# One transformer-like block on one core: early sums on every pair, the last pair behind five chunks, another order in the input norm

## The chip, the cores and the metric

The kernel runs on one core of a Trainium2 chip. The metric is the device time of one execution in microseconds (us); the kernel before takes 1717.28 us, the median of 3 runs (1715.68 to 1718.93).

## What is computed

The input x is a sequence of 1024 tokens of width 1024, in float32. One block is applied:

```
h  = rms_norm(x, norm_mix_g);  proj = h @ w_in            # 4 mixers' inputs, a and b of the delta net, 4 gates
merged = sum over 4 mixers of sigmoid(gate) * (mixer(...) @ w_br)
x  = x + merged @ w_out
h  = rms_norm(x, norm_ffn_g)
up = causal_conv3(h @ w_up) + conv_b;  val, gate = split(up)       # 2 x 2816 channels
x  = x + (silu(gate) * val) @ w_down                               # 2816 -> 1024
out = rms_norm(x, norm_final_g)
```

All matrix products keep float32 accuracy: each operand is split into a rounded high part and the rest (`hi`, `lo`), and every product of two blocks is three matmuls (hi*hi, lo*hi, hi*lo).

## The kernel before

The activations lie with channels on the 128 partitions and tokens along the free dimension, in two halves of 512 tokens (f = 0 and 1). Weights are streamed from memory in pieces of 128x512, 256 KB each, and split on the chip: ScalarE (ACT) makes the high part (L148), VectorE (DVE) or GpSimd (POOL) subtracts to get the low part (L155). Each engine works through its own queue in order. What stands in a queue before what is decided before the run by a list scheduler: of the instructions whose inputs it believes ready it takes the one that comes first in the program. So the order written in the code is a priority, and neighbouring steps are mixed. A queue can therefore hold an instruction that the scheduler thought ready and that is not.

**Input norm** (`norm_in`, L349 to L401). The norm needs the sum of squares of every token, which is late. So the first products run on unnormalised x*g, and their results are scaled afterwards by the row of inverse roots `rt`. For each half f: `scale_split` makes h_hi and h_lo; the products of the first delta-net block (`pd`) and of the 8 columns for a and b (`ab_products`) run; the squares are summed (`ssq`), `rms_scale` reduces them on TensorE and takes the inverse root in some twelve tiny DVE instructions (`rs1m`, `rs1a`, `rs1y` for f = 1); `spread_scale` spreads the result with 8 small matmuls and copies it to `rt` (L404). Two gate blocks are then multiplied (`pg`, `ps`, 24 matmuls each for one half), and `rescale` (L406) rewrites h of a half as the normalised one: eight times a DVE multiplication (L411), a cast on ACT and a subtraction (L155), the latter on DVE for k = 0, 3, 6 and on POOL for the other five. `ab_out` (L422) multiplies the a/b columns by `rt` (L426, tile `abf`), transposes them on TensorE (L96) and adds them up; the delta net's scalars start from that.

**Up projection** (`ffn_up`, L1598). 22 pairs i of blocks (a value block and a gate block), each a 2x2 block product done with seven instead of eight block products (`seven`): 84 matmuls of 512 columns a pair. TensorE writes the quarters of the result to the PSUM tiles `qa` and `qb`, of which there are two sets. Between the products DVE adds snapshots into them (L1587, L1589, L1591); the sixth product of a pair waits for L1587. `pair_weights` prepares the seven weight operands of the next pair, with nine POOL instructions a pair (L1545 to L1552 and L155). `hidden(i)` works on the finished pair: scaling by `rt` (L1617), a 3-tap convolution (L1618, L1620), the gate (L1627, L1628) and the product `val` (L1629), which is stored (`gd[i]`). For the down projection, which is a 2x2 block product with seven products as well, `hidden(i)` also makes sums and stores them: POOL computes and stores one difference of `val` (`td[0]`) for i < 11 and two (`td[1]`, `td[2]`) for i >= 11; and at every even i, with k = i/2, it loads three pieces of the down weights, and POOL computes and stores two sums of them, `sd[0][k]` (L1648) and `sd[1][k]` (L1650). The buffers `tu` for all this are five.

**Down projection** (`ffn_down`, L1677). Seven products of 11 chunks each; a chunk is two pieces of 128x512 (a weight w and a hidden-value piece x), two splits and 12 matmuls. The pieces land in a ring of eight raw slots (`raw_slot`), the split parts go to a ring of seven (`w_slot`, shared with the up projection's weights) or, with `own="t"`, x goes to six tiles of the pool `down`. The pool lies where the up projection's tiles were, so its first use waits until `hidden(21)` and its stores are through. The first product uses rings alone (`own=None`). From the 23rd piece on every even piece has a tile `raws` of the pool `down` (8 of them), and from the second product on x has its own tiles. `residual` loads the x to which the result is added, through POOL's queue. In the program the down projection comes after `hidden(21)`.

Of the kernel before, what the change touches and what calls it, by code (L numbers as in the profile page):

```python
# [21 lines left out]
P = 128  # L22
# [8 lines left out]
LEAD = 24  # L31
N_HELD = 6
# [66 lines left out]
class Builder:  # L99
# [249 lines left out]
    def norm_in(self):  # L349

        nc = self.nc
        with ExitStack() as st:
# [24 lines left out]
            for f, s in enumerate(halves):  # L377
                for k in range(NK):
                    self.scale_split(xs[f][:, k, :], g[:, k:k + 1], self.h_hi[:, k, s], self.h_lo[:, k, s], nc.vector)
                dn.append(self.products(self.early[B_DN], s, self.ps("pd")))  # L380
                ab = self.ab_products(w_ab, s)
                ssq = self.t(xp, [P, 512], F32, "ssq", 2)
                for k in range(NK):
                    x = xs[f][:, k, :]
                    sq = ssq if k == 0 else self.t(xp, [P, 512], F32, "rms_sq", 4)
                    nc.scalar.activation(sq, x, AF.Square)
                    if k:
                        nc.vector.tensor_tensor(ssq, ssq, sq, op=ALU.add)
                r = self.rms_scale(xp, ssq, self.ones, 1.0 / 1024, f"rs{f}")
                self.spread_scale(r, f)  # L390
                if f:
                    self.rescale(xs[0], g, 0)
                o = [self.products(self.early[B_GATE], s, self.gate_ps()), self.products(self.load_in(B_GATE + 1), s, self.ps())]
                if f:
                    self.rescale(xs[1], g, 1)
                for i in range(2):
                    self.gate_out(i, s, self.scaled(o[i], s))
                self.ab_out(xp, ab, s, f)
            self.started = {B_GATE + 2: [self.products(self.load_in(B_GATE + 2), halves[0], self.gate_ps())]}
            self.started[B_DN + 2] = [self.products(self.load_in(B_DN + 2), halves[0], self.ps())]  # L400
# [5 lines left out]
    def rescale(self, x, g, f):  # L406

        nc = self.nc
        s = slice(512 * f, 512 * f + 512)
        for k in range(NK):  # L410
            nc.vector.scalar_tensor_tensor(x[:, k, :], x[:, k, :], g[:, k:k + 1], self.rt[:, s], op0=ALU.mult, op1=ALU.mult)  # L411
            self.split(self.h_hi[:, k, s], self.h_lo[:, k, s], x[:, k, :], nc.scalar, nc.vector if k % 3 == 0 else nc.gpsimd)
# [972 lines left out]
    def build(self):  # L1385
# [44 lines left out]
        with ExitStack() as sx, ExitStack() as st:  # L1430
# [12 lines left out]
            with ExitStack() as s1:  # L1443
                self.ffn_up(ctx, sx, st, s1, xs, ssq, late)
        self.ffn_down(ctx)
# [152 lines left out]
    def ffn_up(self, ctx, sx, st, s1, xs, ssq, late):  # L1598
# [23 lines left out]
        def hidden(i, q):  # L1622
# [20 lines left out]
            if i % 2 == 0:  # L1643
                k = i // 2
# [3 lines left out]
                g.tensor_tensor(a21, a21, a22, op=ALU.add)  # L1648
# [22 lines left out]
        for i in range(1, N_FF):  # L1671
            j = job(i)
            for _ in j[2]:
                pass
            hidden(*j[:2])

    def ffn_down(self, ctx):  # L1677
# [3 lines left out]

        nc = self.nc
        v, g = nc.vector, nc.gpsimd
        pool = self.pool(ctx, "down", side="left")
# [4 lines left out]
        def raw(src):  # L1689
            i = next(n_raw)  # L1690
            r = flat(self.raw_slot("rffsrfsf"[i % 8])) if i < 2 * N_HALF or i % 2 else self.t(pool, [P, 512], F32, "raws", 8)
# [19 lines left out]
        def A(a, b):  # L1711
            return lambda k: self.a["w_dn"][N_HALF * b + k][:, halves[a]]
# [6 lines left out]
        G = [[x[:, h] for x in self.banks() for h in halves] for _ in range(2)]  # L1719
# [75 lines left out]
        product(G[0], [A(0, 0)], [B(0, 0)], True, own=None)  # L1795
        residual(0, 0)
        product(G[1], [A(0, 1)], [B(1, 0)], True, between={5: adds(0, 0, G[0]), 7: lambda: residual(1, 0)})
# [124 lines left out]
```

## Time and profile before

| | before |
|---|---|
| median of 3 runs | 1717.28 us (1715.68 to 1718.93) |
| the profiled execution's own time | 1719.06 us |
| its span, first to last instruction | 1717.3 us |
| TensorE (PE) busy | 1641.2 us, 96% |
| DVE / ACT / POOL busy | 1256.2 / 678.4 / 645.1 us |
| mean granted TensorE clock | 0.984 of full speed |

The profile is of one execution. Busy PE is the time in which a matmul is under way; it contains time at a lower clock. In the lists of instructions a row is start, duration (us), engine, line, operation, output<-inputs, shape, count; what stands in brackets is the idle time of the engine before the instruction and what ended it. A line can be that of a helper: L92 is every matmul, L148 the cast to the high part, L155 the subtraction for the low part.

### The profile page before, as it was taken

The numbers are of one execution on the slowest core, as the hardware profiler recorded it, in microseconds if no ns is written. First come the engines' busy times: TensorE is split into PE (matmuls) and PEld (weight loads), VectorE is DVE, ScalarE is ACT, GpSimd is POOL, SyncE is SP. The second block draws the span as 40 slices with busy tenths as digits, with TensorE's granted clock in tenths as the row PEclk, the third lists the DMA queues.
The fourth block names the chain that finished last, engine by engine and source line by source line (L and its number), as shares of the span: only waits on it lengthen the run. The fifth ranks groups of instructions, "written<-read, shape, count | busy, mean of one in ns | idle before, by whom it ended". The sixth has DMA issues, their size and how long they took to land.

```text
span 1717.3 us, 22540 instructions
## 1 busy us (share of the span) xinstructions
PE 1641.2 (96%) x7762; PEld 1321.3 (77%) x7762; DVE 1256.2 (73%) x2265; ACT 678.4 (40%) x1219; POOL 645.1 (38%) x571
## 2 busy tenths in 40 slices
PE   7899999989999999999999999999998989999996
PEld 5686776766787877778888787788887777778886
DVE  8895966777623749795578667888878888855785
ACT  4342332212332336564213445454443434444353
POOL 2412033344310222211001425988999898300002
PEclk9899999999999999999999999999999999999998
DMA  4113222213432673414755442433344344687763
GB/s 156 66 64 90 60 83 70 90 64 78 149 130 98 137 141 90 102 50 150 275 201 172 141 141 66 143 123 128 135 142 148 135 147 148 219 306 242 246 213 104
DMA packets 137955, 233.64 MB, mean 136 GB/s; under 512 B 42785, under 2 KB 51745, under 8 KB 137329
## 3 DMA queue, kind: packets, MB, share of 16 engines
q1 hardware_dynamic: 105072, 151.26, 28.4%
q10 hardware_dynamic: 17968, 54.37, 8.7%
q0 software_dynamic: 14800, 26.58, 6.0%
q8 instruction: 61, 1.00, 0.2%
q14 instruction: 54, 0.43, 0.1%
HBM read 164.69 MB, written 66.85 MB: 135 GB/s over the span
## 4 chain that ended last, share of the span: by engine, by line
PE 68%; DVE 10%; DMA 3%; issue 3%; POOL 2%; ACT 2%; SPq 0%; DVEq 0%; POOLq 0%; ACTq 0%
PE qb L92 16%; PE pd L92 15%; PE qa L92 14%; PE pg L92 13%; PE ps L92 6%; DVE glo L155 2%; PE ps L96 1%; PE p L92 1%; DVE cg L1628 1%; DMA fr<-sd 1%; DMA fr<-gd 1%; ACT p L1029 0%; DMA raws<-in_w_dn_dram 0%; POOL x L1772 0%; DVE wlo L155 0%
## 5 line engine op out<-in xcount | busy, mean ns | idle before, releaser
L155 POOL TENSOR_TENSOR glo<-raw,ghi 128x512 fp32r<-128x512 f32 x72 | 98.3, 1368 | 361.7 <-ACT ghi L148 348.5
L92 PE MATMUL pg<-hhi,ghi 128*128 128x512 f32 x496 | 207.2, 418 | 0.0
L92 PE MATMUL pg<-hlo,ghi 128*128 128x512 f32 x496 | 198.9, 401 | 0.0
L92 PE MATMUL pg<-hhi,glo 128*128 128x512 f32 x496 | 198.8, 401 | 0.0
L92 PE MATMUL pd<-hhi,whi 128*128 128x512 f32 x312 | 128.2, 412 | 2.0 <-ACT silt L511 1.9
L92 PE MATMUL pd<-hhi,wlo 128*128 128x512 f32 x312 | 122.4, 392 | 2.0 <-DVE wlo L155 2.0
L92 PE MATMUL pd<-hlo,whi 128*128 128x512 f32 x312 | 122.2, 392 | 0.0
L148 ACT CAST ghi<-raw 128x512 fp32r<-128x512 f32 x97 | 59.9, 618 | 152.6 <-DVE cv L1629 75.8
L92 PE MATMUL qa<-xh,ghi 128*128 128x512 f32 x264 | 105.4, 399 | 14.9 <-DVE qa L1587 14.9
L92 PEld LDWEIGHTS pg<-hhi,ghi 128*128 128x128 f32 x496 | 95.1, 192 | 23.1 <-issue 6.7
L92 PEld LDWEIGHTS pg<-hlo,ghi 128*128 128x128 f32 x496 | 95.2, 192 | 19.3
L92 PEld LDWEIGHTS pg<-hhi,glo 128*128 128x128 f32 x496 | 95.5, 192 | 15.8 <-issue 0.3
L92 PE MATMUL qa<-xh,glo 128*128 128x512 f32 x264 | 104.4, 395 | 0.0
L92 PE MATMUL qa<-xl,ghi 128*128 128x512 f32 x264 | 104.3, 395 | 0.0
L92 PE MATMUL qb<-xh,whi 128*128 128x512 f32 x264 | 103.1, 391 | 1.2 <-ACT whi L148 0.8
L92 PE MATMUL qb<-xh,wlo 128*128 128x512 f32 x264 | 102.7, 389 | 0.0
L92 PE MATMUL qb<-xl,whi 128*128 128x512 f32 x264 | 102.7, 389 | 0.0
L148 ACT CAST whi<-raw 128x512 fp32r<-128x512 f32 x90 | 55.9, 621 | 89.2 <-PE pd L92 53.4
L155 DVE TENSOR_TENSOR wlo<-raw,whi 128x512 fp32r<-128x512 f32 x61 | 46.7, 767 | 39.1 <-ACT whi L148 38.9
L92 PEld LDWEIGHTS pd<-hhi,whi 128*128 128x128 f32 x312 | 58.8, 189 | 20.0 <-ACT silt L511 3.8
L1340 ACT ACTIVATE gate<-pg 128x512 f32<-128x512 f32 x62 | 37.1, 599 | 92.5 <-PE pg L92 91.8
L92 PEld LDWEIGHTS qa<-xh,ghi 128*128 128x128 f32 x264 | 50.6, 192 | 27.9 <-DVE qa L1587 17.4
(716 smaller groups left out, 4554.7 us busy)
## 6 DMA issues: line engine op xcount, KB each, us to landing
raw<-in_w_in_dram SPq DMA_DIRECT2D x104, 256.0 KB
gates<-gate ACTq DMA_DIRECT2D x32, 512.0 KB
gld<-gates ACTq DMA_DIRECT2D x32, 512.0 KB
fr<-in_w_up_dram SPq DMA_DIRECT2D x44, 256.0 KB
raw<-in_w_up_dram SPq DMA_DIRECT2D x44, 256.0 KB
gd<-cv ACTq DMA_DIRECT2D x22, 512.0 KB
raws<-in_w_dn_dram SPq DMA_DIRECT2D x44, 256.0 KB
tu<-in_w_dn_dram SPq DMA_DIRECT2D x33, 256.0 KB
```

The source lines that it names most:

```text
L92: return self.nc.tensor.matmul(out, w, x, **kw)
L96: return self.nc.tensor.transpose(out, x, ident)
L148: eng.copy(out, in_)
L155: (e_lo or self.nc.vector).tensor_tensor(lo, src, hi.bitcast(F32), op=ALU.subtract)
L1340: self.nc.scalar.activation(self.gt[i][:, s], ps, AF.Tanh, scale=0.5)
L1628: v.scalar_tensor_tensor(gate, t, 1.0, gate, op0=ALU.add, op1=ALU.mult)
```

## The change

It has four edits. First, the sums of the down weights are made for i < 11 with k = i (the `else` of the test that makes the second difference of `val`) instead of at every even i; so the pairs 0 to 10 have one difference and two sums, the pairs 11 to 21 two differences, and the first of the two sums, a21 + a22, is computed on DVE instead of POOL. Second, `ffn_down` is a generator that is stepped from `ffn_up`: five chunks of its first product come in the program before `hidden(21)`, the other six after it and before the up projection's pools are closed; the pool `down` is opened after that. Third, the raw ring serves the first 44 pieces instead of the first 22, and the second product's x parts go to the ring of split parts (`own=None`). Fourth, in the input norm the first gate block's products come before the spreading of the inverse roots, `rescale` subtracts on DVE alone, and `ab_out` of the second half comes after the products of gate block 2.

```diff
@@ norm_in
                 r = self.rms_scale(xp, ssq, self.ones, 1.0 / 1024, f"rs{f}")
+                o = [self.products(self.early[B_GATE], s, self.gate_ps())]
                 self.spread_scale(r, f)
                 if f:
                     self.rescale(xs[0], g, 0)
-                o = [self.products(self.early[B_GATE], s, self.gate_ps()), self.products(self.load_in(B_GATE + 1), s, self.ps())]
+                o.append(self.products(self.load_in(B_GATE + 1), s, self.ps()))
...
-                self.ab_out(xp, ab, s, f)
+                if f == 0:
+                    self.ab_out(xp, ab, s, f)
             self.started = {B_GATE + 2: [self.products(self.load_in(B_GATE + 2), halves[0], self.gate_ps())]}
+            self.ab_out(xp, ab, s, 1)
@@ rescale
-            self.split(self.h_hi[:, k, s], self.h_lo[:, k, s], x[:, k, :], nc.scalar, nc.vector if k % 3 == 0 else nc.gpsimd)
+            self.split(self.h_hi[:, k, s], self.h_lo[:, k, s], x[:, k, :], nc.scalar, nc.vector)
@@ build
-                self.ffn_up(ctx, sx, st, s1, xs, ssq, late)
-        self.ffn_down(ctx)
+                down = self.ffn_down(ctx)
+                self.ffn_up(ctx, sx, st, s1, xs, ssq, late, down)
+        for _ in down:
+            pass
@@ ffn_up, hidden
-            if i % 2 == 0:
-                k = i // 2
+            else:
                 a21, a22, a11 = (self.t(fp, [P, 512], F32, "tu", 5) for _ in range(3))
...
-                g.tensor_tensor(a21, a21, a22, op=ALU.add)
+                v.tensor_tensor(a21, a21, a22, op=ALU.add)
@@ ffn_up
             for _ in j[2]:
                 pass
+            if i == N_FF - 1:
+                next(down)
             hidden(*j[:2])
+        next(down)
@@ ffn_down
-        pool = self.pool(ctx, "down", side="left")
-            r = flat(self.raw_slot("rffsrfsf"[i % 8])) if i < 2 * N_HALF or i % 2 else self.t(pool, [P, 512], F32, "raws", 8)
+            r = flat(self.raw_slot("rffsrfsf"[i % 8])) if i < 4 * N_HALF or i % 2 else self.t(pool, [P, 512], F32, "raws", 8)
-        G = [[x[:, h] for x in self.banks() for h in halves] for _ in range(2)]
+        G = [[x[:, h] for x in self.banks() for h in halves]]
-        product(G[0], [A(0, 0)], [B(0, 0)], True, own=None)
+        for k in range(N_HALF):
+            if k == EARLY:
+                yield
+            run(G[0], parts([A(0, 0)(k)]), parts([B(0, 0)(k)]), k == 0, k == N_HALF - 1)
+        yield
+        G.append([x[:, h] for x in self.banks() for h in halves])
+        pool = self.pool(ctx, "down", side="left")
         residual(0, 0)
-        product(G[1], [A(0, 1)], [B(1, 0)], True, between={5: adds(0, 0, G[0]), 7: lambda: residual(1, 0)})
+        product(G[1], [A(0, 1)], [B(1, 0)], True, own=None, between={5: adds(0, 0, G[0]), 7: lambda: residual(1, 0)})
```

`EARLY` is 5 and `N_HALF` is 11.

## Rows read from the trace of the kernel before

**Rows 1.** The page, part 1: busy time and share of TensorE.
```profile
PE 1641.2 (96%) x7762; PEld 1321.3 (77%) x7762; DVE 1256.2 (73%) x2265; ACT 678.4 (40%) x1219; POOL 645.1 (38%) x571
```

**Rows 2.** Windows of the span: length, busy us (x instructions) by engine, PEclk, DMA share, GB/s.
```profile
1097.00:1306.00 209.00, 209.00 (x924) 173.06 (x923) 169.03 (x143) 99.70 (x143) 189.59 (x144) 1.00 0.40 135
1306.00:1344.00 38.00, 33.30 (x138) 27.03 (x137) 31.24 (x22) 16.18 (x23) 30.80 (x27) 0.91 0.42 141
1344.00:1382.00 38.00, 36.39 (x161) 29.82 (x160) 31.13 (x26) 17.56 (x26) 35.36 (x29) 1.00 0.35 126
1382.00:1421.00 39.00, 33.87 (x141) 27.53 (x140) 31.12 (x22) 14.03 (x20) 35.83 (x30) 0.91 0.43 148
1421.00:1459.00 38.00, 36.38 (x160) 29.54 (x159) 31.74 (x26) 16.29 (x25) 31.32 (x27) 1.00 0.50 164
1477.80:1514.80 37.00, 32.95 (x134) 25.54 (x133) 26.61 (x32) 16.64 (x28) 7.41 (x9) 0.95 0.78 257
```

**Rows 3.** Waits, 1290 to 1520 us: us in total, times, longest.
```profile
PE qa L92 <- DVE qa L1587: 13.1, 4, 5.1
```

**Rows 4.** Instructions in order of time, DVE and POOL, 1315 to 1325 us.
```profile
1315.01 7.39 DVE L1628 SCALAR_TENSOR_TENSOR cg<-ct,cg 128x1024 f32<-128x1024 f32 x1
1324.53 0.69 DVE L1587 TENSOR_TENSOR qa<-qa,snap 128x512 f32<-128x512 f32 x1
...
1315.05 1.30 POOL L1550 TENSOR_TENSOR fs<-raw,fr 128x512 f32<-128x512 f32 x1
...
1320.04 1.27 POOL L155 TENSOR_TENSOR wlo<-fs,whi 128x512 fp32r<-128x512 f32 x1
1321.39 2.13 POOL L1545 TENSOR_TENSOR fs<-fr,fr 128x512 f32<-128x512 f32 x1
```

**Rows 5.** Groups of DVE and POOL instructions, 1097 to 1306 us.
```profile
L1628 DVE SCALAR_TENSOR_TENSOR cg<-ct,cg 128x1024 f32<-128x1024 f32 x11 | 22.4, 2038 | 1.4 <-ACT ct L1627 1.4
...
L1649 POOL DMA_DIRECT2D sd<-tu x5 | 2.8, 558 | 1.5 <-POOL tu L1648 1.5
```

**Rows 6.** Groups of DVE instructions, 1513 to 1717 us.
```profile
L1708 DVE TENSOR_TENSOR raws<-raws,fr 128x512 f32<-128x512 f32 x17 | 11.7, 688 | 7.2 <-DMA fr<-sd 5.0 <-DMA fr<-in_w_dn_dram 2.1
```

**Rows 7.** In order of time: DVE and the first matmul of one pair's sixth product.
```profile
1109.43 0.69 DVE L1587 TENSOR_TENSOR qa<-qa,snap 128x512 f32<-128x512 f32 x1
...
1110.96 0.39 PE L92 MATMUL qa<-xh,ghi 128*128 128x512 f32 x1
```

**Rows 8.** In order of time, 1500 to 1510 us: SP's queue, ACT, PE.
```profile
1500.44 0.93 SPq L1692 DMA_DIRECT2D fr<-gd  x2
...
1507.62 1.14 ACT L148 CAST th<-fr 128x512 fp32r<-128x512 f32 x2 [6.37 <-DMA fr<-gd]
...
1509.18 0.61 ACT L148 CAST whi<-fr 128x512 fp32r<-128x512 f32 x1
...
1509.85 0.50 PE L92 MATMUL qa<-whi,ghi 128*128 128x512 f32 x1 [3.48 <-ACT whi L148]
```

**Rows 9.** Waits of TensorE, 20 to 80 us.
```profile
PE ps L92 <- DVE rs1y L236: 3.4, 1, 3.4
PE ps L96 <- DVE abf L426: 3.2, 1, 3.2
```

**Rows 10.** Narrow windows after three waits (columns as in rows 2).
```profile
54.20:59.90 5.70, 5.70 (x18) 4.83 (x19) 2.50 (x4) 2.28 (x4) 1.19 (x1) 0.50 0.06 22
71.40:77.60 6.20, 6.20 (x18) 4.92 (x19) 4.87 (x31) 2.42 (x5) 0.00 (x0) 0.53 0.88 290
1367.40:1370.00 2.60, 2.57 (x11) 2.15 (x12) 1.30 (x2) 0.96 (x2) 2.52 (x3) 1.00 0.60 226
```

**Rows 11.** Groups of DVE and POOL instructions of the rescaling, 37 to 72 us.
```profile
L411 DVE SCALAR_TENSOR_TENSOR x<-x,cols,rt 128x512 f32<-128x512 f32 x16 | 16.7, 1082 | 2.8 <-ACT rt L404 2.8
L155 DVE TENSOR_TENSOR hlo<-x,hhi 128x512 fp32r<-128x512 f32 x6 | 6.8, 1130 | 0.5 <-ACT hhi L148 0.5
...
L155 POOL TENSOR_TENSOR hlo<-x,hhi 128x512 fp32r<-128x512 f32 x10 | 16.4, 1663 | 19.1 <-PE ps L92 13.0 <-ACT hhi L148 6.1
```

More of the change, by code (lines that the diff above doesn't have):

```diff
@@ L31 @@
 LEAD = 24
+EARLY = 5
 N_HELD = 6
@@ L1595, in banks, with ffn_up @@
         return [self.t(self.pp, [P, L], F32, x, 2) for x in ("qa", "qb")]
-    def ffn_up(self, ctx, sx, st, s1, xs, ssq, late):
+    def ffn_up(self, ctx, sx, st, s1, xs, ssq, late, down):
         nc = self.nc
```

## The prediction

> **What bounds the kernel.** I read the page's busy times first. TensorE is busy 1641.2 of 1717.3 us [rows 1], so what a change gives is the time in which TensorE waits or runs slowly, 76 us of idle and some more of low clock. Then I cut the span into windows and looked for the stages in which it is not at its pace. The reader is to see the pace in the first window of [rows 2]: 924 matmuls, eleven pairs of 84, in 209.00 us without a gap, 0.2262 us each. Set against that, a window's length minus its count times 0.2262 is what it loses, idle and low clock together:
>
> - 1306 to 1344: 38.0 - 138 x 0.2262 = 6.8; 1344 to 1382: 1.6; 1382 to 1421: 7.1; 1421 to 1459: 1.8. These four hold the pairs 14, 16, 18 and 20, and lose 17.3 together [rows 2].
> - 1477.8 to 1514.8, the first product of the down projection: 37.0 - 134 x 0.2262 = 6.7 [rows 2].
> - In the input norm two waits, 3.4 and 3.2 [rows 9], each followed by some 6 us at the lower of the two clock levels: 0.50 for 5.7 us and 0.53 for 6.2 us, so 2.85 and 2.9 more [rows 10]. Together 12.3.
>
> The list of waits then gives the names: in the pairs TensorE waited four times, 13.1 us in total, for the DVE instruction L1587 [rows 3]. The order of time says why L1587 was late. In front of it DVE had L1628, which took 7.39 us from 1315.01; POOL ran five instructions from 1315.05 to 1321.31 with no gap between them, and L1628 ended about one instruction's time after the first gap (the next POOL instruction starts at 1321.39) [rows 4]. The same group takes 2.04 us in the mean between 1097 and 1306, where nothing is lost [rows 5]. So DVE is locked out by an unbroken run of POOL, and only where POOL has more to do than a pair lasts.
>
> **Sums on every pair.** Before, hidden(i) for even i >= 12 puts four arithmetic instructions on POOL (two differences, two sums), for odd i >= 11 two; even i < 11 three, odd one. After, each has two. The five late even pairs lose two of 1.30 us [rows 4] and the two stores of 0.56 behind them [rows 5], and become like the odd ones, after which no stall follows. I take away the whole 17.3. Added are eleven DVE sums of two SBUF tensors of 128x512, 0.69 each by the same kind of instruction [rows 6], 7.6 us of DVE work. DVE works 169 of 209 us in those pairs [rows 2], so there is room, but the place matters: the sum comes in the program before the next pair's L1587, and behind L1587 stand TensorE's sixth product and all later DVE work. L1587 ends at 1110.12 and the product starts at 1110.96 [rows 7], 0.84 us of cover. An undisturbed sum fits (0.69); behind one POOL instruction it would be 0.69 + 1.30 - 0.84 = 1.15 late, 12.7 for eleven. I take 0.05 each, 0.6 in all, since DVE also idles while it waits for other matmuls and the scheduler can use that. The three loads move from even pairs to all of the first eleven; they stand in SP's queue ahead of weight pieces, need four of the five tu buffers a pair instead of five in the even ones, and the write that frees a buffer is a pair old by then: nothing. Term: -17.3 + 0.6 = -16.7, between -17.3 and -4.6.
>
> The row says that DVE stays out for five POOL instructions in a row [rows 4]. The Trainium skill (SBUF — State Buffer, "Who interferes with whom") says that a DVE instruction with two SBUF inputs and a reading GpSimd instruction exclude each other, and that the one that came second is blocked until the first is finished. Taken by the letter, that is one POOL instruction of 1.30, not 6; a shorter queue on POOL would then not mend L1628. That is a rival below.
>
> **Last pair behind five chunks.** In the trace of before the loss of this stage lies late: TensorE waits 3.48 us at 1509.85 for the cast of the eleventh chunk's x [rows 8]. That cast stood in ACT's queue behind two casts `th` of the next product, and those waited 6.37 us for two loads issued at 1500.44 and landed 7 us later [rows 8]. The scheduler had put them first because they had buffers of their own. With the second product in the same ring of split parts, its parts can't overtake the first's. So the 3.48, the low clock behind it and the small waits about it go. What stays: DVE still does hidden(21) while the chunks need their splits, and DMA is at 0.78 in this stage [rows 2]. Putting five chunks first changes little by itself, since the scheduler already mixed chunks and hidden(21). The ring leaves three and a half chunks of lookahead, 3.5 x 12 x 0.2262 = 9.5 us, above the 7 us of the slow load. Late next is the same kind of overtaking at the border of the second and third product, where x again gets tiles of its own; it needs a load as slow as those, and the burst of loads at the opening of the pool is then over. I leave 2.3 of the 6.7. Term: -4.4, between -6.7 (nothing waits) and +6.7 (nothing goes, and the next border costs the same again).
>
> **Input norm.** First wait: TensorE had done most of the first gate block of half 1 when the spreading matmuls, queued before its last four matmuls, made it wait 3.4 for the roots [rows 9]. Now all 24 come first: 0.9 us of work in the gap. The roots come earlier too, since POOL's ten subtractions (16.4 us) go to DVE: the six that DVE had took 1.13 each and its multiplications 1.08 [rows 11], against 0.69 for such an instruction left alone [rows 6]. As an estimate from these rows, DVE's part is 16 x 0.7 + 16 x 0.69 = 22.2 instead of 16.7 + 6.8 = 23.5, and what it has is not lengthened by locks. So sixteen subtractions cost DVE what six and the locks did, and the tiny instructions of the roots don't wait for POOL. I leave 1.5 of the 3.4; after a wait of 1.6 TensorE was granted the full clock [rows 10], so the 2.85 goes as well: -4.75. Second wait: eight more matmuls of gate block 2 come before the transposes (1.8 us) so the 3.2 would shrink to 1.4. But DVE has 8 multiplications, 8 subtractions, two scaled outputs and `abf` after the roots, 19 x 0.69 = 13.1, and TensorE's two blocks of 24 matmuls are over in 10.9: 2.2 of wait stay. With full clock after it the gain is 3.9 of 6.1, with the low clock once more 1.0; I take 1.75, nearer to the low one. Term: -6.5, between -12.3 and +3 (ten more subtractions are 6.9 in DVE's path, and of the lock time, 6 x 0.44 + 16 x 0.38 = 8.7, only half comes back).
>
> **Sum.** -16.7 - 4.4 - 6.5 = -27.6. The profiled execution took 1719.06, which is 1.78 above the median of the runs; 1719.06 - 27.6 = 1691.5, and on the scale of the median 1689.7. Forecast: 1690.
>
> **Rivals.**
> (a) Only the pairs gain. The overtaking moves to the next border and the input norm is DVE bound, so the waits there change place. For it: DVE's full load in both, and that a new program makes a new list. Against it: the waits have named causes that go. 1717.3 - 16.7 = 1701.
> (b) The lock ends with each POOL instruction, and L1628 was long for another cause that stays. Then the pairs keep their 17.3: 1717.3 - 10.9 + 0.6 = 1707. Against it stand the five gapless instructions and the end right after [rows 4].
> (c) Slower. The new DVE sum is itself caught by a run of POOL, as L1628 was: about 6.2 us of wait, 0.69 of work, 0.84 of cover and some 2.2 of low clock make 8.2 a pair. From four of the eleven pairs on the gain of 27.6 is gone; with seven, 1717.3 + 57.4 - 27.6 = 1747. For it: L1629 sets POOL's differences free at the moment when the sum would run. And POOL, at 189.6 of 209 in the first eleven pairs [rows 2], gets some ten more stores of 0.56 there [rows 5]. Against it: those are 0.5 a pair of the 1.8 that POOL has free, its arithmetic there stays at two instructions a pair on average, and each pair's run has ended in time so far.
> (d) The scheduler orders DVE and TensorE much as before and later stages shift their small waits against each other: no change.
>
> **Chances.** Forecast 0.69 (its own range 1684 to 1696), (a) 0.17, (b) 0.05, (c) 0.06, (d) 0.03. A measurement of this kernel tells 0.2% from no change, 3.4 us. Faster by more than that: 0.69 + 0.17 + 0.05 = 0.91; within it 0.03; slower 0.06. The range reaches from all three terms in full (-36.3: 1681) to the pairs alone with 6 us of lost cover (-11: 1706).
>
> **What would show it.** Right: L1628 at about 2 us in all pairs, the windows of pairs 14 to 20 at 0.2262 us a matmul, the first eleven pairs still without a gap, no cast of a later product in front of an earlier one in ACT's queue, the clock at full speed at 55 and 72 us. Wrong: gaps before the sixth product in pairs 1 to 11 (then c), long L1628 in the late pairs although POOL has less to do (b), waits of the same size at the next border or behind `abf` (a).

## The result, and the profile after

The changed kernel takes 1693.43 us (median of 4 runs, 1689.32 to 1693.47); the kernel before, beside it, 1717.78 (4 runs). The ratio is 0.9854, 95% interval 0.9836 to 0.9871: 24 us faster, where 1690 was forecast, with a range of 1681 to 1706. The profiled execution took 1693.45 with a span of 1691.7 and a mean clock of 0.993.

To see where the time went I put the two traces side by side by the number of matmuls done, not by time. The gap between them is 7.5 us when the up projection starts, 22.1 when it ends, 25.1 after the second product of the down projection, and 25.6 at the last matmul. Lines have moved by 6 to 8: L1587, L1589, L1591, L1628 are L1593, L1595, L1597, L1634; the new sum is L1653.

Page part 1 of the changed kernel, TensorE's row, against [rows 1]: the same 7762 matmuls are busy for 10 us less, which I take for clock won back; the rest of the gain is idle time.
```profile
PE 1631.1 (96%) x7762; PEld 1312.2 (78%) x7762; DVE 1243.7 (74%) x2286; ACT 677.6 (40%) x1219; POOL 622.0 (37%) x550
```

Windows of the changed kernel, against [rows 2], cut at pair and product borders: eight pairs (3 to 10, after 1089.86), pair 11, two of the stages of two late pairs, then the first and the second product of the down projection. Columns as in [rows 2].
```profile
1089.86:1244.65 154.79, 154.74 (x673) 125.53 (x672) 133.55 (x112) 72.39 (x105) 150.65 (x113) 1.00 0.48 163
1244.65:1265.26 20.61, 19.35 (x86) 15.69 (x84) 16.65 (x14) 9.32 (x14) 20.07 (x17) 1.00 0.53 179
1303.34:1341.42 38.08, 38.08 (x170) 31.54 (x168) 30.02 (x26) 18.14 (x27) 33.27 (x26) 1.00 0.35 121
1379.50:1417.58 38.08, 38.08 (x170) 31.54 (x168) 31.17 (x26) 18.13 (x27) 33.20 (x27) 1.00 0.36 124
1455.66:1485.58 29.92, 29.92 (x134) 24.78 (x132) 22.63 (x27) 14.12 (x22) 5.53 (x6) 1.00 0.70 228
1485.58:1519.62 34.04, 31.12 (x134) 24.46 (x132) 18.19 (x32) 14.65 (x27) 1.41 (x2) 1.00 0.77 254
```

A pair at TensorE's pace is 19.04 us. The late pairs are all at it now: two take 38.08, where the four stages of [rows 2] lost 17.3. The instruction that stood locked out in pairs 14 and 18, L1628 before and L1634 after, over the late pairs (shortest, median and longest in ns):
```profile
L1628 DVE SCALAR_TENSOR_TENSOR cg<-ct,cg x9: 1210/2181/7386, 1295.5 to 1466.5; 128x1024 f32<-128x1024 f32 x9
L1634 DVE SCALAR_TENSOR_TENSOR cg<-ct,cg x9: 1224/2196/2236, 1292.0 to 1444.4; 128x1024 f32<-128x1024 f32 x9
```
In pairs 16 and 20 it was the subtraction in front of L1628 (4.57 and 4.58 us). Pair 16 before:
```profile
1358.83 4.57 DVE L155 TENSOR_TENSOR glo<-fs,ghi 128x512 fp32r<-128x512 f32 x1 [0.41 <-ACT ghi L148]
```
By matmul counts pairs 14, 16, 18 and 20 are 7.18, 1.90, 7.44 and 2.13 shorter, 18.65 together. But eight early pairs take 154.79 instead of 152.32, 0.31 each more, and pair 11 takes 1.57 more: 4.05 given back. The first down product is at its pace, 29.92 against 37.02 (-7.10); the second takes 34.04 against 29.96 (+4.08). The input norm's part is below.

What costs the early pairs 0.31 is seen in order of time, in pair 7: DVE, then POOL (start, duration, idle time before in brackets).
```profile
1182.27 0.85 DVE L1653 TENSOR_TENSOR tu<-tu,tu 128x512 f32<-128x512 f32 x1 [0.84 <-DMA tu<-in_w_dn_dram]
1183.04 0.69 DVE L1595 TENSOR_TENSOR qb<-qb,snap 128x512 f32<-128x512 f32 x1
...
1180.85 1.72 POOL L1551 TENSOR_TENSOR fs<-fr,fr 128x512 f32<-128x512 f32 x1
1182.53 1.73 POOL L1640 TENSOR_TENSOR tu<-cv 128x512 f32<-128x512 f32 x1
```
The sum stands in DVE's queue behind L1593 and ahead of L1595, which TensorE's next product needs. It waits for its loads until 1182.27 and ends at 1183.12, 0.55 us after POOL's L1551 (1182.57); L1595 starts right behind, and TensorE's next two matmuls come 0.16 and 0.11 late. In each of the pairs 3 to 10 the sum ends 0.55 after L1551. In pair 11 its loads come 1.63 late, it is caught by the instruction behind L1551, L1640, and the pair loses 1.57.

What costs the second product 4.08, in order of time: SP's queue, ACT, TensorE.
```profile
1477.71 0.80 SPq L1700 DMA_DIRECT2D raws<-sd  x2
...
1480.52 0.47 SPq L1700 DMA_DIRECT2D fr<-in_w_dn_dram  x1
...
1486.11 2.45 SPq L1700 DMA_DIRECT2D raws<-sd  x2
...
1490.11 0.62 ACT L149 CAST ghi<-fr 128x512 fp32r<-128x512 f32 x1 [8.86 <-DMA fr<-in_w_dn_dram]
...
1491.30 0.50 PE L93 MATMUL qa<-whi,ghi 128*128 128x512 f32 x1 [2.84 <-ACT whi L149]
```
ACT waits 8.86 us for a piece issued at 1480.52, which is there 9.6 later; the ring held 9.5 us of work. SP issued pieces of the third product (`raws<-sd`) before and after it, and POOL two loads of the residual (512 KB each).

The waits of the input norm, against [rows 9], and two windows behind the two waits that end at 55.09 and 67.17, against [rows 10]:
```profile
PE pg L93 <- ACT gate L1344: 1.6, 1, 1.6
PE ps L93 <- DVE rs1y L237: 1.2, 1, 1.2
```
```profile
55.09:61.00 5.91, 5.91 (x30) 5.05 (x31) 4.65 (x8) 3.60 (x6) 0.00 (x0) 1.00 0.29 93
67.17:73.00 5.83, 5.83 (x27) 4.60 (x28) 5.38 (x27) 2.41 (x5) 0.00 (x0) 1.00 0.73 240
```
Waits of 1.2 and 1.6 stand where 3.4 and 3.2 stood, and the full clock follows both. That the first wait is shorter is not because the roots come earlier. The last of the tiny instructions, before and after, and the spreading behind it:
```profile
53.88 0.16 DVE L236 SCALAR_TENSOR_TENSOR rs1y<-rs1a,rs1y 128x4 f32<-128x4 f32 x1
```
```profile
54.78 0.16 DVE L237 SCALAR_TENSOR_TENSOR rs1y<-rs1a,rs1y 128x4 f32<-128x4 f32 x1
55.09 1.13 PE L93 MATMUL ps<-consts,rs1y 128*128 128x128 f32 x8 [1.23 <-DVE rs1y L237]
```
The roots are 0.9 later; TensorE has 31 gate matmuls to do ahead of them instead of 20: the four that stood behind the spreading, and seven of the next gate block, whose rescaled h was ready in time.

The two kernels do the matmuls of this stretch in another order, so the gap is read only where both have done the same ones: the changed kernel is 0.5 behind at 49 us, 8.9 ahead at 181, 7.2 at 291 and 7.5 at the up projection. The eight kernels of this study with the changed norm (e6 left out) are 6.3 to 9.3 ahead of the profile before at 181 us and 4.9 to 8.9 at 291; those with the old norm -0.9 to 1.0 and -0.1 to 1.8. So the gain is the norm's, and a single profile is uncertain by some 2 us. Between there and the up projection more scatter comes on: the kernels whose code up to there is the changed kernel's start it between 1023.9 and 1030.1 (this one 1024.4).

### The profile page after: what moved, and what is told of

It is laid out like the page before. It is cut to its first block, busy times and chain, and to the rows that moved or that the text cites. A ratio compares the mean times of both kernels' runs of the same rounds, so it can differ in the third digit from the quotient of the medians.

```text
span 1691.7 us, 22545 instructions
## 1 busy us (share of the span) xinstructions
PE 1631.1 (96%) x7762; PEld 1312.2 (78%) x7762; DVE 1243.7 (74%) x2286; ACT 677.6 (40%) x1219; POOL 622.0 (37%) x550
## 4 chain that ended last, share of the span: by engine, by line
PE 66%; DVE 12%; POOL 11%; issue 4%; DMA 4%; ACT 2%; SPq 0%; POOLq 0%; DVEq 0%; ACTq 0%
PE pd L93 19%; PE pg L93 15%; PE qb L93 12%; PE qa L93 10%; PE ps L93 8%; POOL wlo L156 3%; POOL glo L156 2%; PE ps L97 2%; PE p L93 1%; DMA fr<-in_w_dn_dram 1%; POOL tu L1640 1%; POOL fs L1551 1%; POOL fs L1558 1%; POOL tu L1655 1%; POOL fs L1553 1%
## 5 line engine op out<-in xcount | busy, mean ns | idle before, releaser
L156 POOL TENSOR_TENSOR glo<-raw,ghi 128x512 fp32r<-128x512 f32 x72 | 99.0, 1378 | 386.7 <-ACT ghi L149 368.3
L156 DVE TENSOR_TENSOR wlo<-raw,whi 128x512 fp32r<-128x512 f32 x63 | 47.2, 751 | 39.6 <-ACT whi L149 39.2
L156 POOL TENSOR_TENSOR wlo<-fs,whi 128x512 fp32r<-128x512 f32 x42 | 66.6, 1586 | 9.6 <-ACT whi L149 9.2
```

Of the source, the lines that this page charges most:

```text
L156: (e_lo or self.nc.vector).tensor_tensor(lo, src, hi.bitcast(F32), op=ALU.subtract)
```

## The experiments

Twelve kernels; the kernel before ran beside each (medians 1716.66, 1718.56, 1718.49 and 1718.41 us). Ratios are to it, with 95% intervals. Lengths of pairs and products are by matmul counts from each profile.

| kernel | median us (runs) | ratio |
|---|---|---|
| e1, sums alone | 1702.98 (5) | 0.9914 [0.9898, 0.9930] |
| e2, down projection's edits alone | 1719.64 (12) | 1.0013 [1.0000, 1.0026] |
| e3, input norm alone | 1711.63 (12) | 0.9963 [0.9951, 0.9976] |
| e4, early sum back on POOL | 1702.80 (4) | 0.9916 [0.9901, 0.9930] |
| e5, two raws buffers | 1723.14 (10) | 1.0028 [1.0010, 1.0045] |
| e6, rescaling back on POOL | 1699.36 (4) | 0.9895 [0.9866, 0.9924] |
| e7, no ring for product two | 1690.71 (4) | 0.9842 [0.9804, 0.9880] |
| e8, before, POOL's run broken | 1704.75 (8) | 0.9928 [0.9906, 0.9949] |
| e9, six tu buffers | 1694.85 (4) | 0.9868 [0.9830, 0.9905] |
| e10, sum behind L1597, no ring | 1694.69 (4) | 0.9862 [0.9843, 0.9882] |
| e11, before with the ring alone | 1715.09 (10) | 0.9988 [0.9977, 0.9999] |
| e14, half of the sums on POOL, no ring | 1701.53 (6) | 0.9901 [0.9876, 0.9926] |

### Each edit by itself

**e1**, the kernel before with the first edit:
```diff
-            if i % 2 == 0:
-                k = i // 2
+            else:
...
-                g.tensor_tensor(a21, a21, a22, op=ALU.add)
+                v.tensor_tensor(a21, a21, a22, op=ALU.add)
```


> The kernel before with the first edit alone (sums for i < 11, first sum on DVE). Theory: an unbroken run of POOL instructions locked DVE out of L1628 in the late pairs, and POOL had more work than a pair lasts only behind the even hidden(12) to hidden(18); so pairs 14, 16, 18 and 20 come to 19.04 us each (they gain 18.7 together), and the new DVE sum costs 0.3 in each of pairs 3 to 10 and 1.6 in pair 11 (4.1 together): 14.6 us less than before, about 1703. Rival: the stalls went in the changed kernel because the whole program was scheduled anew; then single pairs still stall here and the gain is under 10 us.

Measured 13.7 us less than before. The late pairs give the same 18.65, the pairs 3 to 11 take back 4.96 (0.1 to 0.35 in most, 1.57 and 1.75 in pairs 7 and 9), and the first down product keeps its loss (36.54). The theory holds in the sums, not pair by pair, and this edit carries more than half of the gain.

**e2**, the kernel before with `ffn_down` as a generator, five chunks ahead of `hidden(21)`, and the ring for 44 pieces:
```diff
+            if i == N_FF - 1:
+                next(down)
             hidden(*j[:2])
+        next(down)
```


> The kernel before with the down projection's edits alone (five chunks ahead of the last pair, ring for the first 44 pieces, second product's x in the ring). Theory: first product without a stall, 29.9 us instead of 37.0; second product 34.0 instead of 30.0, because the pieces of the third product are loaded ahead into free tiles and crowd the ring's loads: 3 us less, about 1714. Rival: the freed POOL in the last pairs was needed for it (hidden(20) has four POOL instructions here): then the first product keeps 2 to 4 us of its loss and the sum is about 0.

No gain in time. The profile says why: product one goes from 37.02 to 29.92 as the theory had it, product two from 29.96 to 37.84 (34.0 expected), where TensorE waits 4.7 for a cast of ACT. The stall was moved, not removed.

**e3**, the kernel before with the fourth edit, that of the input norm:
```diff
+                o = [self.products(self.early[B_GATE], s, self.gate_ps())]
                 self.spread_scale(r, f)
...
-            self.split(..., nc.scalar, nc.vector if k % 3 == 0 else nc.gpsimd)
+            self.split(..., nc.scalar, nc.vector)
```


> The kernel before with the input norm's edits alone. Theory: the two waits of 3.4 and 3.2 us and their low clock shrink as in the changed kernel, matmuls at 180 us are 5.2 us earlier and the first matmul of the up projection 7.5 us earlier: about 1710. Rival: the 2.3 us that came between 180 and 1030 us are chance of the new schedule and not of the norm; then the up projection starts 5 us earlier, about 1712.

Measured 5.0 less; waits of 1.6 and 1.2 as in the changed kernel, and 7.8 ahead at 181 us, 6.6 at 291.

### The norm: order or engine

**e6**, the changed kernel with POOL's subtractions back:
```diff
-            self.split(..., nc.scalar, nc.vector)
+            self.split(..., nc.scalar, nc.vector if k % 3 == 0 else nc.gpsimd)
```


> The changed kernel with five of each eight subtractions of the input norm's rescaling back on POOL, so that of the third edit only the new order of the matmuls stays. Theory: both parts are needed; the order gives TensorE 0.9 us of work ahead of the first wait and 1.8 ahead of the second, and the roots come earlier only because DVE's small instructions no longer wait for POOL. Then the first wait for the roots is 2 to 3 us instead of 1.2, the second 2 to 3 instead of 1.6, one of them is followed by the low clock again, and of the 5.2 us that the norm gained by 180 us some 2 are left: about 3 us above the changed kernel's 1693.4. Rival: the order alone does it: waits and clock as in the changed kernel, and the time within 1 us of it.

The waits of TensorE in e6, 20 to 80 us, and the window behind the longest:
```profile
PE ps L93 <- DVE rs1y L237: 3.5, 1, 3.5
...
PE ps L97 <- DVE abf L430: 1.6, 1, 1.6
```
```profile
56.03:61.00 4.97, 4.97 (x19) 4.16 (x20) 3.08 (x5) 2.73 (x5) 0.56 (x1) 0.66 0.13 46
```
The first wait is back in full, with the lower clock behind it (0.66 over 4.97 us), although the four matmuls stand ahead of it: 24 are done before it, but none of the next gate block. The second is halved, as in the changed kernel. So the engine is worth the first wait and the order the second: where the same matmuls are done, at 181 us, e6 is 4.1 ahead of the kernel before, the changed kernel 8.9. At 291 us it is 0.3 and 7.2; e6 has a wait of 2.8 for a load in between, and why only there stays open. (The time of e6, 5.9 above the changed kernel's, holds more: its second down product took 35.84, and its up projection began late.) The group rows show the engine's part:
```profile
L415 DVE SCALAR_TENSOR_TENSOR x<-x,cols,rt 128x512 f32<-128x512 f32 x16 | 17.9, 1151 | 2.0 <-ACT rt L408 2.0
```
In the changed kernel, with POOL out of the way, the same sixteen take 11.3:
```profile
L415 DVE SCALAR_TENSOR_TENSOR x<-x,cols,rt 128x512 f32<-128x512 f32 x16 | 11.3, 744 | 1.3 <-ACT rt L408 1.3
```

### The lock

By the lock I mean that a DVE instruction and a POOL one don't run together, and one of them waits. **e8**, the kernel before with two one-element writes by POOL in each pair:
```diff
+        if not first:
+            g.memset(s3[:, 0, 0:1], 0.0)
         g.tensor_tensor(s3, a11, a21, op=ALU.subtract)
...
+            g.memset(s4[:, 0, 0:1], 0.0)
         g.tensor_tensor(s4, a12, s2, op=ALU.subtract)
```


> The kernel before, with a one-element write by POOL ahead of two of its subtractions of each pair after the first (the element is overwritten), so that POOL has two more instructions a pair that read no SBUF tensor, and the run of five reading instructions without a gap is broken. Theory: DVE stays out for as long as POOL's readers follow each other without a gap. Then L1628's 7.4 us in the pairs 14, 16, 18 and 20 falls to 3 to 5, and the four windows there lose 6 to 14 instead of 17.3; the time is 3 to 10 us under the kernel before. Rival, which is (b) of the prediction: DVE gets its turn after each POOL instruction anyhow, and L1628 was long because POOL had too much to do before it was released; two more POOL instructions then change nothing or cost a little: L1628 stays at 7.4, the windows lose 17 to 20, 1717 to 1722.

In order of time in pair 14, DVE and POOL, against [rows 4]:
```profile
1315.90 1.21 DVE L1632 SCALAR_TENSOR_TENSOR cg<-ct,cg 128x1024 f32<-128x1024 f32 x1
1317.14 2.20 DVE L1633 TENSOR_TENSOR cv<-cv,cg 128x1024 f32<-128x1024 f32 x1
...
1315.90 0.12 POOL L1551 MEMSET fs<- 128x1 f32 x1
1316.11 2.16 POOL L1552 TENSOR_TENSOR fs<-raw,fr 128x512 f32<-128x512 f32 x1
```
L1632 is the old L1628. With a write of 0.12 us at the head of POOL's run, DVE is first, takes 1.21 instead of 7.39, and POOL's instruction is the one that is stretched (2.16). Pair 14 loses nothing, the pairs 14 to 21 lose 6.5 in all where they lost 18.65 (of TensorE's waits there 3.0 are for POOL's low parts, 0.7 for L1591), and the time falls by 13.8, more than the 3 to 10 expected. POOL had more to do than before, and two thirds of the loss went: rival (b) is refuted by the chip.

The Trainium skill (SBUF — State Buffer, "Who interferes with whom") says that the order of issue, not the shape of the operation, decides which of the two is blocked. This trace agrees on the shape: the same pair of instructions is 7.39 and 1.30 one way [rows 4], 1.21 and 2.16 the other. That the order of issue decides can't be read from the recorded starts: in [rows 4] L1628 starts 0.04 us ahead of POOL's L1550 and is the one that is blocked.

### The early sum

**e4**, the changed kernel with the sum on POOL again, in all eleven pairs:
```diff
-                v.tensor_tensor(a21, a21, a22, op=ALU.add)
+                g.tensor_tensor(a21, a21, a22, op=ALU.add)
```


> The changed kernel with the first sum back on POOL (still for i < 11). Theory: the 0.3 us a pair come from DVE, which waits in order for the sum's loads ahead of L1595; without it pairs 3 to 10 fall to 19.04 and pair 11 loses its 1.6, 4.1 us less, about 1689. Rival: POOL then has three instructions and three stores in each of the eleven pairs, more than a pair lasts, its runs have no gap, and DVE is locked out as before: stalls of 2 to 7 us in several early pairs, 1700 or more.

From pair 7 on 0.91 to 1.54 is lost in every pair, 8.2 over the pairs 3 to 12. The theory falls; the rival's time came, though with smaller stalls than its 2 to 7 us. DVE was the cheaper place.

**e9**, the changed kernel with six tu buffers:
```diff
-            t = self.t(fp, [P, 512], F32, "tu", 5)
+            t = self.t(fp, [P, 512], F32, "tu", 6)
```


> The changed kernel with six tu buffers instead of five; the order of DVE and of SP's issues is the same, only the loads of the early sums can start sooner. Theory: pairs 3 to 11 take 19.35 us instead of 19.04, and pair 11 1.57 more, because the new DVE sum L1653 stands ahead of the next pair's L1595 and waits 0.2 to 1.6 us for its loads, which wait for a tu buffer. Then L1653 no longer waits for DMA, the nine pairs go back to 19.04 to 19.1, and the time is 3 to 4 us below the changed kernel's 1693.4: about 1690. Rival: POOL, 97% busy in these pairs, sets the 19.35 itself, since it computes the values that the pair needs and now issues the sums' stores in every pair: the pairs stay at 19.35 with six buffers and the time at 1693, with pair 11's 1.3 gone at most.

The pairs 3 to 10 stay at 19.30 to 19.45, pair 11 at +1.59: the theory falls. SP issues the loads no sooner, since what stands ahead of them is a weight piece that waits for POOL and DVE to free its slot, not for a tu buffer. And where the loads are in time the sum is no earlier. Pair 7 of e9:
```profile
1181.17 1.63 DVE L1653 TENSOR_TENSOR tu<-tu,tu 128x512 f32<-128x512 f32 x1
...
1180.52 1.73 POOL L1551 TENSOR_TENSOR fs<-fr,fr 128x512 f32<-128x512 f32 x1
```
It starts without a wait, is shut out by L1551 until 1182.25, and ends 0.55 later, as in the changed kernel. The recorded wait for the loads hid the lock.

**e10**, the changed kernel without the ring, and with the sum tied to L1597 of the next pair:
```diff
+                v.tensor_scalar(one, q[0][:, 512:513], 0.0, 1.0, op0=ALU.mult, op1=ALU.add)
+                v.scalar_tensor_tensor(a21, a21, one, a22, op0=ALU.mult, op1=ALU.add)
```


> A version meant to beat both: the changed kernel without the ring (the second product's parts in their own buffers) and with the early sum made to stand behind L1597 of the next pair on DVE: its scalar operand, a one, is made by a 128x1 instruction from that result. Theory: the early sum cost pairs 3 to 10 0.31 us each and pair 11 1.57 because it stood ahead of L1595, for which TensorE waits, either waiting for its loads or shut out by one POOL instruction. Behind L1597 DVE has 1.1 us of idle time until TensorE's last product, so the nine pairs go back to 19.04 (4.05 less), and the second product stays at 30.1 (3.9 less): 1693.4 - 8.0 = 1685.5. Rival: L1623 behind it frees the next pair's banks and comes 0.8 us later, and POOL's difference of the early sum comes later too, so that another wait takes the place: pairs at 19.2 to 19.6 still, and only the ring's 3.9 gained: 1689 to 1690.

The pairs 3 to 12 take 19.90: worse than TensorE's pace by 0.86 each, and both readings set down before fall short. Pair 6, DVE and POOL:
```profile
1170.54 2.17 DVE L1660 SCALAR_TENSOR_TENSOR tu<-tu,one,tu 128x512 f32<-128x512 f32 x1
1172.63 1.22 DVE L1623 TENSOR_TENSOR qa<-qa,rt 128x1024 f32<-128x1024 f32 x1
...
1170.85 1.31 POOL L156 TENSOR_TENSOR wlo<-fs,whi 128x512 fp32r<-128x512 f32 x1
```
The idle 1.1 us was real, but the sum is caught there as well: 2.17 us, ending 0.55 after POOL's L156. L1623 and all behind it come later, and TensorE waits 0.56 for L1593. The second product, without the ring, took 29.98.

**e14**, the changed kernel without the ring, the sums of even pairs on POOL:
```diff
-                v.tensor_tensor(a21, a21, a22, op=ALU.add)
+                (v if i % 2 else g).tensor_tensor(a21, a21, a22, op=ALU.add)
```


> The changed kernel without the ring, and with the early sums of the even pairs (six) on POOL, where they were before, and only those of the odd pairs (five) on DVE. Theory: what the early sums cost is paid where DVE's sum is shut out by POOL's instruction ahead of L1595, 0.31 us each, so only the odd pairs pay; an even pair with its sum on POOL lost nothing before. The pairs 3 to 12 then lose 1.5 instead of 4.05, the late pairs stay at 19.04, the second product at 30: 1693.4 - 2.5 - 4 = 1687. Rival: POOL was 97% busy with two instructions less in the even pairs, and with its differences and stores in every pair six sums more put it over what a pair lasts: the even pairs then lose 0.9 or more, as with all sums on POOL, and the time is 1691 to 1695.

Slower than either said. Of the pairs 3 to 11 three are at 19.04, four at 19.33 to 19.49, and pairs 4 and 8 take 26.75 and 23.80. Pair 4, SP, DVE and POOL:
```profile
1124.67 1.32 SPq L1652 DMA_DIRECT2D tu<-in_w_dn_dram  x3
...
1131.77 1.77 DVE L1653 TENSOR_TENSOR tu<-tu,tu 128x512 f32<-128x512 f32 x1 [4.67 <-DMA tu<-in_w_dn_dram]
1133.46 0.68 DVE L1595 TENSOR_TENSOR qb<-qb,snap 128x512 f32<-128x512 f32 x1
...
1131.71 1.27 POOL L156 TENSOR_TENSOR wlo<-fs,whi 128x512 fp32r<-128x512 f32 x1
```
The loads were issued 0.55 us before L1593 started (1125.22), in the changed kernel's pair 7 2.8 before (1176.77 and 1179.55): SP's queue waited for slots that POOL, with a third arithmetic instruction in the even pairs, freed later (12.0 us for L1556, 10.8 in the changed kernel). DVE stood 4.67 us in front of the sum, TensorE 4.98 for L1595, and the clock was 0.50 for the next 5.7 us:
```profile
1134.20:1139.90 5.70, 5.70 (x13) 4.47 (x14) 1.95 (x3) 1.37 (x2) 5.58 (x6) 0.50 0.24 92
```
The pair's loss, 7.7, is about what rival (c) gave a caught pair (8.2), by another road: the wait was for loads, not for the lock.

### The down projection: chunks first, or the ring

**e7**, the changed kernel without the ring:
```diff
-            ... if i < 4 * N_HALF or i % 2 else self.t(pool, [P, 512], F32, "raws", 8)
+            ... if i < 2 * N_HALF or i % 2 else self.t(pool, [P, 512], F32, "raws", 8)
...
-        product(G[1], [A(0, 1)], [B(1, 0)], True, own=None, between={...})
+        product(G[1], [A(0, 1)], [B(1, 0)], True, between={...})
```


> The changed kernel with the second product's parts in buffers of their own again (and its pieces loaded as before), so that the five chunks stand first but the ring ends with product one. Theory: the loss of the first product before the change (37.0 against 29.9 us) came from parts of the second product that were cast ahead of the first's. Then the first product is again 35 to 37 us here with a cast of the second in front of one of the first on ACT, the second about 30, and the time 1 to 4 us above the changed kernel's 1693.4 (the second product's own 4.1 comes back against it): 1694 to 1697. Rival: the five chunks put first are what removed it; the first product stays at 30, and the second loses its 4.1 no longer: about 1689.

**e11**, the kernel before with the ring alone: the same two lines the other way.

> The kernel before with the ring alone: the second product of the down projection takes its parts from the first's ring and its pieces from the same slots; the last pair's values stay ahead of the chunks, as before. Theory, as the prediction had it: parts of the second product cast ahead of the first's are the cause, so the ring alone takes the first product from 37.0 to about 30, and the second pays 4 to 8 as it did in the changed kernel and in the second edit alone: 1714 to 1719. Rival, which the kernel without the ring speaks for: the place of the five chunks is what counts; with the ring alone the first product stays at 35 to 38, and the time at 1717 or above.

The windows of the first and second product, e7, then e11:
```profile
1457.61:1487.53 29.92, 29.92 (x134) 24.77 (x133) 22.54 (x27) 14.64 (x23) 5.54 (x6) 1.00 0.66 221
1487.53:1517.66 30.13, 30.13 (x134) 24.70 (x132) 22.23 (x41) 16.19 (x31) 2.83 (x4) 1.00 0.97 348
```
```profile
1476.46:1507.40 30.94, 30.80 (x134) 24.54 (x132) 23.65 (x27) 13.84 (x22) 7.48 (x9) 1.00 0.81 270
1507.40:1541.31 33.91, 32.09 (x133) 25.80 (x132) 18.34 (x32) 14.78 (x27) 1.42 (x2) 0.95 0.76 256
```
Either is enough for the first product: the chunks without the ring, in the changed kernel, give 7.10, the ring alone 6.08 (e1 keeps the loss, so the first edit is not what removed it in e7). For the second product the ring is what costs: with it the product loses 4 to 8 (34.04, 37.84, 33.91 and, in e4, e6 and e9, 34.3 to 35.8), without it nothing (30.13 here, 29.98 in e10, 29.92 in e14). The rival of e7 holds: the chunks remove the loss without the ring, and the ring brings the second product's.

But e7's theory had one thing right: the casts still overtake. Of the first product's casts the last, `whi<-fr`, stands behind two of the second product's pieces on ACT:
```profile
1479.65 0.62 ACT L149 CAST th<-fr 128x512 fp32r<-128x512 f32 x1 [1.89 <-DMA fr<-gd]
1481.57 0.62 ACT L149 CAST ghi<-raws 128x512 fp32r<-128x512 f32 x1 [1.30 <-DMA raws<-in_w_dn_dram]
1482.10 0.62 ACT L149 CAST whi<-fr 128x512 fp32r<-128x512 f32 x1
```
Here it costs nothing, since `th` waits 1.89 for its load, where it waited 6.37 before [rows 8]. Its load was issued at 1475.65, ahead of the pool's first loads (`raws` at 1478.77, the residual's at 1478.99); before the change at 1500.44, behind them (1498.69 and 1499.22). So the loss took both, the overtaking cast and its late load; that the place behind the other loads made it late fits these times and was not tried alone.

**e5**, the changed kernel with two raws buffers:
```diff
-            ... self.t(pool, [P, 512], F32, "raws", 8)
+            ... self.t(pool, [P, 512], F32, "raws", 2)
```


> The changed kernel with two raws buffers instead of eight, so that SP can bring only two pieces of the third product's sd sums ahead of the second product's weight pieces. Theory: in the changed kernel the second product of the down projection took 34.04 us instead of 29.92 because this prefetch (six pieces and two x2d loads between 1477.7 and 1486.1) made the weight piece issued at 1480.52 land 9.6 us later, as long as the ring looks ahead. Then the second product takes 30 to 31 us here, no wait of TensorE above 0.5 us at its fourth chunk, and the time is 3 to 4 us below the changed kernel's 1693.4: about 1690. Rival: the residual loads and the DVE additions alone starve it, or the third product then waits for its own pieces: the second product stays at 33 to 34, or the third grows by what the second gains; 1693 to 1695.

The second product went from 34.04 to 32.32 only, the third to 30.89, and the fifth and sixth, whose pieces no longer came ahead, to 41.49 and 44.63. So the prefetch of the third product's pieces explains 1.7 of the 4.1 at most; how the rest divides between the residual's loads, the additions on DVE and the short ring stays open. The time, 1723.14, is far above what either theory or rival had: neither looked as far as the fifth product.

## Why the prediction was right, point by point

- **Bound.** Right: the gain is idle time and low clock of TensorE in the places named.
- **Late pairs.** -17.3 predicted, -18.65 measured. The cause is shown by e8 and not only argued: DVE shut out by POOL. The prediction blamed L1628 for all four pairs. That holds for 14 and 18; in pairs 16 and 20, which lose 1.9 and 2.1, L1628 takes 1.21 and the subtraction in front of it is shut out (4.57 and 4.58). The prediction had DVE locked out until POOL leaves a gap. The runs show less: either engine may be the one that waits. In the early pairs DVE was let in after one POOL instruction with no gap behind it (L1551 and L1640 above), in [rows 4] only after five. What decides that stays open.
- **Sum on DVE.** Mis-sized: 0.6 predicted, 4.05 measured. The step that failed is the one that let the sum fit into the 0.84 us of cover with 0.05 each; and the sum stands ahead of L1595, the old L1589, not ahead of the old L1587 for which that cover was read. The bound named beside it, caught by one POOL instruction, is what happens in nearly every early pair, though it costs 0.31 there and not 1.15, since only the rest of that instruction is waited for. And "nothing" for the three loads was wrong in kind: they stand in SP's queue behind pieces that wait for POOL, and in e14 loads that came late by this made TensorE wait 4.98 and 3.26. Rival (c) did not happen in the changed kernel; losses of its size came in e14, by late loads and not by the lock.
- **Transition.** -4.4 predicted, -7.10 + 4.08 = -3.0 measured. Right in part: the ring keeps the second product's casts from overtaking, and with it alone the loss goes (e11). But overtaking is not the whole cause; in e7 it is still there and costs nothing. Wrong twice: "putting five chunks first changes little by itself" (it removes all of it, e7), and the 9.5 us of lookahead, which were to be above the slowest load: a load of 9.6 came. What was to be late next, casts at the border of the second and third product, did not come; the loss was inside the second product. That -3.0 lies near -4.4 is in part luck: a larger gain and a loss in a place not foreseen.
- **Norm.** -6.5 predicted, -8.9 by 181 us and -7.2 by 291 us in the changed kernel. The waits left are 1.2 and 1.6, where 1.5 and 2.2 were forecast, with the full clock behind both. "The roots come earlier too" is wrong: they come 0.9 later, and the first wait shrank because seven matmuls of the next gate block were ready as well. The second is not for `abf` but for a gate tile that ACT frees. That DVE's own time would fall without POOL is shown: 17.9 to 11.3 for the multiplications (e6 and the changed kernel).
- **Sum.** -27.6 predicted, -25.6 between the two profiled executions: 7.5 up to the up projection, 18.65 - 4.05 in it, 3.0 in the down projection, 25.1 together, and 0.5 behind the last product. That the total came so near is in part luck too: the late pairs and the norm gave some 1.3 and 1.0 more than forecast, the DVE sums and the transition 3.5 and 1.4 less. The edits alone give 13.7, 5.0 and -3.0 by their medians, 15.7 together, less than the 24; part of it is the second product, 37.84 in e2 and 34.04 in the changed kernel, the rest I can't assign.

No version run here is clearly better than the changed kernel. e7 has the lowest median (1690.71), and its second product is 3.9 us shorter; its interval overlaps the changed kernel's, so the gain is shown by the stage and not by the time.

## What to carry to other kernels

A new instruction is not priced by its duration and the engine's free time, but by what stands behind it in the queue and by which engine may shut it out where it stands: 0.69 us of work cost 0.31 a pair in one place, 0.86 in a better looking one, and 5 us where its loads came late. When two remedies for one stall go in together, run each alone: here either was enough, and one of them cost 4 us one stage later. A recorded wait can hide another limit that ends at the same time; moving the wait (e9) is how to find out.

## What was not expected of the hardware

A DVE sum of two tensors in SBUF, the on-chip memory, that was shut out by POOL ended 0.55 us after the end of the POOL instruction in each case looked at (1182.57 to 1183.12, 1182.25 to 1182.80, 1172.16 to 1172.71, 1132.98 to 1133.54), whatever its start. And a load of 256 KB took 9.6 us to be usable in a stretch where the DMA engines moved 316 GB/s in the mean (1475 to 1490 us): ten pieces and two loads of 512 KB, 3.7 MB, had been issued between 1477.7 and 1483.2.
